# S5 output products on two halves of 64 rows, and the low weight halves of xBC and z on VectorE

## The chip, the cores and the metric

The kernel runs on one core of one Trainium2 chip. The metric is the device time of one execution in microseconds (us). Three runs of the kernel before took 1704.28, 1708.3 and 1718.86 us, so the median is 1708.3 us. The profiled execution, from which all rows below come, took 1714.9 us. Engines are named as the profile names them: PE (TensorE), DVE (VectorE), ACT (ScalarE), POOL (GpSimd) and SP (SyncE, which here only issues DMAs). Batch numbers, where the text uses them, count from 0.

## The reference, cut to what matters

One layer of a hybrid encoder on 1024 tokens of width 1024. A projection splits into z, xBC, dt and u. The columns z, xBC and dt feed a Mamba-2 group (SSD), u feeds an S5 group with 64 groups of 16 channels and 64 complex states in each direction. The two outputs are concatenated, projected, normed and added, and a SwiGLU layer follows. The change lies in the projection and the S5 part:

```
def _s5_scan(ug, lam_re, lam_im, log_dt, b_re, b_im, c_re, c_im):
    ...
    bu_re = jnp.einsum("blgh,gph->blgp", ug, bb_re)
    bu_im = jnp.einsum("blgh,gph->blgp", ug, bb_im)
    ...
    _, _, h_re, h_im = lax.associative_scan(_complex_linear_combine,
                                            (a_re, a_im, bu_re, bu_im), axis=1)
    return jnp.einsum("blgp,ghp->blgh", h_re, c_re) - jnp.einsum("blgp,ghp->blgh", h_im, c_im)

def _s5_mixer(u, ...):
    y_f = _s5_scan(ug, lam_re[0], ...)
    y_b = jnp.flip(_s5_scan(jnp.flip(ug, 1), lam_re[1], ...), 1)
    y = (y_f + y_b).reshape(bsz, seq, D_S5) + d_skip * u
    g = jax.nn.gelu(y)
    return g * jax.nn.sigmoid(g @ glu_w + glu_b)
```

## The kernel before, in words

Every large product is done in three products of split operands: a weight block `raw` of 128 x 1024 is split into a high half `whi` (a cast on ACT, L265) and a low half `wlo` (a subtraction, L266), and `gemm` runs high by high, high by low and low by high, 48 matmuls of 512 columns for a block of 128 output channels. Where the subtraction runs is set by the string `pl` in the table `KN`: it holds X and Z, so the 12 xBC blocks and the 8 z blocks take it on POOL, all others on DVE. `ensure(i + 1)` at the head of each block emits the split of the block after it.

S5 is done in chunks of 8 tokens, so the scan has 128 chunks (index k). `s_batch` makes the chunk inputs of all groups and writes them into the tile `SH` (L559). `rec_step(j)` (L617 to L629) then runs the recurrence over chunks, for both directions at once: four DVE instructions of 128 elements per row (`rn`, `rm`, `rn`, `SH`), each step on the result of the step before, 127 steps. SH is laid out with the chunk outside and the 64 values of a chunk (two components, 32 groups) next to each other. Its rows hold two groups of 64 states each (j = 0, 1).

While the recurrence runs, a loop over 18 blocks (9 of xBC, one of dt, 8 of z) emits for each block: the split of the next one, the matmuls, 8 recurrence steps, a piece of the convolution (`conv_taps`, four DVE instructions at L722, and `conv_silu` on ACT), and near the end of the loop the first pieces of the S5 output stage. All of this is under a manual schedule: each engine executes its instructions in the order in which the code emits them.

The S5 output stage (the loop over i in 16 batches of 4 groups, behind the recurrence) gives each batch three products per group, summed in PSUM (`y_mm`, L778 to L780): the within-chunk kernel `W0` times the input U, and the carried states of each direction times `cp`. The pieces are:

- `c_open`, `c_dir` (L663 to L673): cp, the output matrix times powers of the diagonal. For the first four batches on POOL (`pcd`), later on DVE.
- `k_mm`, `k_out` (L690 to L698): the within-chunk kernel, from cp and `yk`; it is copied by ACT to `lg`, gets the skip term on POOL, and goes to DRAM (`k_d`).
- `w0_load` (L704): reads it back in Toeplitz form into W0. These DMAs, and those into k_d, are issued on POOL's queue.
- `restack` (L768): a product over 128 rows needs both components of one group in the rows, and SH has two groups there. Eight copies per batch (seven on ACT, one on DVE for the first 11 batches) move SH into the tile `AH`, 128 copies in all.
- `y_out`, `g_store`: GELU on ACT, and the result to DRAM (`g_d`), from which the GLU product behind it reads.

Of the kernel before, what the change touches and what calls it, by code (L numbers as in the profile page):

```python
# [18 lines left out]
def _ap(t, off, dims):  # L19
# [63 lines left out]
 'pl': 'XZ',  # L83
# [47 lines left out]
def hymba_block(ctx, tc, P, out, dbg=None, upto=99):  # L131
# [44 lines left out]
    y12_d = dram([2, 128, 2, 1024 + 16], "y12_d")  # L176
    x12_d = dram([2, 128, 1024], "x12_d")
    k_d = dram([32, 64 * 240], "k_d")
# [110 lines left out]
    arR = rep.tile([128, 8, 128], F32, name="arR")  # L289
    aiR = rep.tile([128, 8, 128], F32, name="aiR")  # L290
# [117 lines left out]
    def s5_prep():  # L408
# [43 lines left out]
        for j in range(2):  # L452
            sl = slice(64 * j, 64 * j + 64)
            srcr = arR[sl, 7, :].rearrange("p (d q j) -> p d q j", d=2, j=2)[:, :, :, j]
# [28 lines left out]
        zp = pp.tile([128, 16], F32, name="zp")  # L483
        pool.memset(zp, 0.0)
        for y in range(2):
# [10 lines left out]
            gq.dma_start(y12_d[y][:, :, 0:1024], st.rearrange("p d g h -> p d (g h)"))  # L496
            with tc.issue_after(pows[7].ins):
                gq.dma_start(y12_d[y][:, :, 1024:1040], zp.unsqueeze(1).to_broadcast([128, 2, 16]))
# [5 lines left out]
        for y in range(2):  # L504
            st = pp.tile([128, 64, 16], F32, tag="n5", name="xst")
            for q in range(2):
                t = ptmp()
                for j in range(8):
                    h = 8 * q + j
                    pe.transpose(t[:, 64 * j:64 * j + 64], cc[:, h, y:y + 2, :].rearrange("p a b -> p (a b)"), ident[:64, :64])  # L510
                act.copy(st[:, :, 8 * q:8 * q + 8].rearrange("p g h -> p h g"), t.rearrange("p (h g) -> p h g", h=8))
            (gq if KN['xq'] else aq).dma_start(x12_d[y], st.rearrange("p g h -> p (g h)"))
# [17 lines left out]
    def s_batch(b, U):  # L530
# [12 lines left out]
        for hb in range(2):  # L543
# [6 lines left out]
            for q in range(2):  # L550
                t = ptmp()
                for d in range(2):
                    for comp in range(2):
                        for j in range(2):
# [4 lines left out]
                act.copy(SH[:, :, :, :, pq].rearrange("p d k c -> p d c k"),  # L559
                         t.rearrange("p (d c k) -> p d c k", d=2, c=2))  # L560
# [83 lines left out]
    def xt_load(b):  # L644
        if b in xts_:
            return
        g0 = 4 * b
        xt = xts_[b] = ck.tile([128, 2, 4, 16], F32, tag="xtc", name="xtc", bufs=2)
        (gq if b < KN["xtb"] else sp).dma_start(xt.rearrange("p y g h -> p y (g h)"), x12_d.rearrange("y p f -> p y f")[:, :, 16 * g0:16 * g0 + 64])
        yk = yks[b] = ck.tile([128, 2, 80], F32, tag="yk", name="yk", bufs=3)  # L650
        (gq if b < KN["xtb"] else sp).dma_start(yk, y12_d[0][:, :, 16 * g0:16 * g0 + 80])

    @pri("cb")
    def c_batch(b):
        c_open(b)
        for d in range(2):
            c_dir(b, d)

    def c_open(b):
        xt = xts_[b]  # L660
        pl = (ck, 4) if b % 7 < 4 else (yp, 3)
        cp = cps[b] = pl[0].tile([128, 2, 4, 9, 16], F32, tag="cp", name="cp", bufs=pl[1])
        act.copy(_ap(cp, 0, [[576 + 128, 2], [144, 4], [1, 16]]), xt[:, 0].unsqueeze(1).to_broadcast([128, 2, 4, 16]))  # L663

    def c_dir(b, d):
        g0 = 4 * b
        e = pool if 2 * b + d in KN['pcd'] else dve
        xt, cp = xts_[b], cps[b]
        tm = ck.tile([128, 4, 8, 16], F32, tag="tmc", name="tmc")
        dst = _ap(cp, 16 if d == 0 else 576 + 112, [[144, 4], [16 if d == 0 else -16, 8], [1, 16]])  # L670
        e.tensor_tensor(dst, spread(xt[:, 0], 8), pw4(arR, d, 1, 8, g0, 4), op=MUL)
        e.tensor_tensor(tm, spread(xt[:, 1], 8), pw4(aiR, d, 1, 8, g0, 4), op=MUL)
        e.tensor_tensor(dst, dst, tm, op=ADD)  # L673
# [3 lines left out]
    @pri("kb")  # L677
    def k_batch(b):
        k_mm(b)
        k_out(b)  # L680

    def k_mm(b):
        yk = yks[b]
        cp = cps[b]
        t = kts[b] = ptmp()
        for g in range(4):
            y0, y1 = yk[:, 0, 16 * g:16 * g + 32], yk[:, 1, 16 * g:16 * g + 32]
            for o, n, st, rhs, a, z in ((0, 8, y1, cp[:, 1, g, 1:9], True, False), (7, 1, y0, cp[:, 0, g, 0:1], False, True),
                                        (8, 7, y0, cp[:, 0, g, 1:8], True, True)):
                pe.matmul(t[32 * g:32 * g + 32, 16 * o:16 * o + 16 * n], st, rhs.rearrange("p n h -> p (n h)"),  # L690
                          start=a, stop=z, tile_position=(0, 32 * g))

    def k_out(b):
        g0 = 4 * b
        lg = ck.tile([128, 15, 16], F32, tag="lg", name="lg", bufs=2)
        act.copy(lg.rearrange("p n h -> p (n h)"), kts[b][:, 0:240])
        pool.tensor_tensor(lg[:, 7, :], lg[:, 7, :], dd[:, b, :], op=ADD)
        gq.dma_start(k_d[:, 240 * g0:240 * g0 + 960].rearrange("h (g f) -> g h f", g=4), lg.rearrange("p n h -> p (n h)"))  # L698
# [52 lines left out]
    AHs = []  # L751

    @pri("rs")
    def restack(b):

        while len(AHs) < 2:
            AH = yp.tile([128, 2, 4, 128], F32, name=f"AH{len(AHs)}")
            pool.memset(AH[:, 0, :, 0:1], 0.0)
            pool.memset(AH[:, 1, :, 127:128], 0.0)
            AHs.append(AH)  # L760
        AH, p0 = AHs[b % 2], 2 * b
        for d in range(2):
            for j in range(2):
                for comp in range(2):
                    src = SH[64 * j:64 * j + 64, d, (0 if d == 0 else 1):(127 if d == 0 else 128), comp, p0:p0 + 2]
                    dst = AH[64 * comp:64 * comp + 64, d, :, (1 if d == 0 else 0):(128 if d == 0 else 127)]
                    dst = dst.rearrange("p (q j) k -> p q j k", j=2)[:, :, j, :].rearrange("p q k -> p k q")
                    (dve.tensor_copy if 4 * d + 2 * j + comp >= 8 - KN["rsd" if b < 11 else "rse"] else act.copy)(dst, src)  # L768

    yts = {}  # L770

    def y_mm(b):
        U, W0, cp, AH = Us_[b // 2], W0s[b], cps[b], AHs[b % 2]
        c = b % 2
        t = yts[b] = ptmp()
        for g in range(4):
            o = t[:, 128 * g:128 * g + 128]
            pe.matmul(o, W0[:, 240 * g:240 * g + 128], U[:, 4 * c + g, :], start=True, stop=False)  # L778
            pe.matmul(o, cp[:, 0, g, 1:9, :].rearrange("p n h -> p (n h)"), AH[:, 0, g, :], start=False, stop=False)
# [1185 lines left out]
```

## Time and profile before

| What | Value |
|---|---|
| median of three runs | 1708.3 us (1704.28 to 1718.86) |
| profiled execution: time, span from the first to the last instruction | 1714.9 us, 1713.2 us |
| PE, PE weight loads | 91% and 74% of the span |
| DVE, ACT, POOL | 74%, 42% and 34% of the span |
| granted TensorE clock, mean | 0.956 of full speed |
| last recurrence step begins, last S5 output product begins | 444.4 us, 551.0 us |

How to read it: the shares are means over stages that differ. PE is the busiest engine overall, but in the two stages of the change, the recurrence (from 212.0 us) and the S5 output stage behind it, other engines can set the pace, and those stages must be read by themselves.

### The profile page before, as it was taken

How to read it: one execution, taken by the hardware profiler on the slowest of the kernel's cores; microseconds unless marked ns; L12 is line 12 of the kernel's file. 1: busy time of each engine (PE TensorE's matmuls, PEld its weight loads, DVE VectorE, ACT ScalarE, POOL GpSimd, SP SyncE). 2: the span in 40 equal slices, each digit the busy share in tenths (PEclk: the TensorE clock that was granted, in tenths of full speed). 3: DMA queues.
4: the chain of work that ended last, by engine and by line, in shares of the span. 5: the costliest groups of instructions: out<-in, count | busy, mean ns of one | idle time of the engine just before them, and what ended most of it. 6: DMA issues, size and time to landing. Idle time of an engine off the chain costs nothing.

```text
span 1713.2 us, 22320 instructions
## 1 busy us (share of the span) xinstructions
PE 1560.2 (91%) x7980; PEld 1272.9 (74%) x7980; DVE 1268.8 (74%) x2012; ACT 712.4 (42%) x1182; POOL 579.3 (34%) x517
## 2 busy tenths in 40 slices
PE   7998999889776879999999986999999999999897
PEld 6777788668675666778877774788888888787686
DVE  7445589999762577877577499878688788669777
ACT  6345632121697445444343255322222233344352
POOL 2101121156121020112111176545555555229512
PEclk9999999989898889999999898999999999999999
DMA  5644344243687748777578891323332231592234
GB/s 179 155 119 116 116 151 136 80 128 108 149 211 170 212 128 274 242 242 254 176 233 276 270 282 56 117 93 119 122 105 99 92 105 55 184 344 80 92 104 179
DMA packets 250146, 272.13 MB, mean 159 GB/s; under 512 B 29403, under 2 KB 190675, under 8 KB 250035
## 3 DMA queue, kind: packets, MB, share of 16 engines
q1 hardware_dynamic: 224659, 216.48, 41.2%
q0 software_dynamic: 12896, 33.83, 6.2%
q10 hardware_dynamic: 12480, 20.39, 3.4%
q8 instruction: 63, 1.03, 0.3%
q14 instruction: 48, 0.39, 0.1%
HBM read 185.76 MB, written 84.84 MB: 158 GB/s over the span
## 4 chain that ended last, share of the span: by engine, by line
PE 40%; DVE 10%; DMA 8%; issue 3%; POOL 3%; ACT 2%; SPq 0%; DVEq 0%; POOLq 0%; ACTq 0%
PE acc L1548 13%; PE ptmp L1548 9%; PE acc L1135 4%; PE ptmp L1852 4%; PE acc L1852 3%; DVE dop L1834 2%; PE acc L275 2%; DMA m<-m_d 2%; POOL wd L1819 1%; PE ptmp L954 1%; DMA m_d<-m 1%; PE ptmp L1020 1%; DMA cat<-ch_d 1%; PE ptmp L1006 1%; DMA graw<-g_d 1%
## 5 line engine op out<-in xcount | busy, mean ns | idle before, releaser
L275 PE MATMUL acc<-hTh,whi 128*128 128x512 f32 (+1 forms) x456 | 180.6, 397 | 8.2 <-ACT whi L265 8.0
L1135 PE MATMUL acc<-ohi,cat 128*128 128x512 f32 x512 | 176.3, 411 | 11.0 <-DMA cat<-ch_d 7.6
L275 PE MATMUL acc<-hTh,wlo 128*128 128x512 f32 (+1 forms) x456 | 179.3, 394 | 2.4 <-POOL wlo L266 2.3
L275 PE MATMUL acc<-hTl,whi 128*128 128x512 f32 (+1 forms) x456 | 180.2, 396 | 0.8 <-DVE hTl L335 0.8
L1531 DVE TENSOR_TENSOR wop<-rawp,wop 128x512 fp32r<-128x512 f32 x120 | 135.1, 1127 | 22.2 <-ACT wop L1530 21.1
L1548 PE MATMUL ptmp<-T,wop 128*128 128x512 f32 x528 | 127.8, 398 | 7.1 <-DVE T L1705 4.7
L1548 PE MATMUL acc<-T,wop 128*128 128x512 f32 x528 | 127.9, 398 | 3.7 <-DVE T L1705 3.7
L1852 PE MATMUL ptmp<-dop 128*128 128x512 f32 x528 | 123.9, 396 | 2.9 <-DVE dop L1834 2.9
L1135 PEld LDWEIGHTS acc<-ohi,cat 128*128 128x128 f32 x512 | 100.2, 196 | 35.0 <-DMA cat<-ch_d 8.5
L266 POOL TENSOR_TENSOR wlo<-raw,whi 128x1024 fp32r<-128x1024 f32 x20 | 50.1, 2505 | 221.2 <-ACT whi L265 221.1
L1548 PE MATMUL acc<-B,wop 128*128 128x512 f32 x528 | 124.3, 391 | 0.0
L1548 PEld LDWEIGHTS ptmp<-T,wop 128*128 128x128 f32 x528 | 101.1, 192 | 30.1 <-DVE T L1705 5.1
L1548 PEld LDWEIGHTS acc<-T,wop 128*128 128x128 f32 x528 | 100.9, 192 | 27.1 <-DVE T L1705 4.5
L1852 PEld LDWEIGHTS ptmp<-dop 128*128 128x128 f32 x528 | 101.5, 193 | 24.9 <-DVE dop L1834 3.2
L1548 PEld LDWEIGHTS acc<-B,wop 128*128 128x128 f32 x528 | 99.0, 188 | 21.5
L275 PEld LDWEIGHTS acc<-hTh,whi 128*128 128x128 f32 x456 | 87.5, 192 | 27.2 <-ACT whi L265 8.4
L1834 DVE TENSOR_TENSOR dop<-da,dop 128x512 fp32r<-128x512 f32 x77 | 76.7, 996 | 38.9 <-ACT dop L1833 38.9
L1563 ACT ACTIVATE cg<-cg 128x512 f32<-128x512 f32 x44 | 27.8, 633 | 185.1 <-DVE cg L1561 185.1
L1569 POOL TENSOR_TENSOR cg<-cg 128x512 f32<-128x512 f32 x44 | 62.0, 1409 | 125.5 <-DVE cg L1564 124.8
L275 PEld LDWEIGHTS acc<-hTh,wlo 128*128 128x128 f32 x456 | 87.3, 191 | 22.2 <-POOL wlo L266 4.2
L1135 PE MATMUL acc<-olo,cat 128*128 128x512 f32 x256 | 103.6, 405 | 0.0
L1530 ACT CAST wop<-rawp 128x512 fp32r<-128x512 f32 x120 | 70.3, 615 | 76.6 <-POOL rawp L1505 51.0
(365 smaller groups left out, 3601.8 us busy)
## 6 DMA issues: line engine op xcount, KB each, us to landing
ff_d<-cg POOLq DMA_DIRECT2D x77, 256.0 KB, 2.3
da<-ff_d SPq DMA_DIRECT2D x35, 512.0 KB
raw<-in_w_in_dram SPq DMA_DIRECT2D x28, 512.0 KB
cat<-ch_d SPq DMA_DIRECT2D x48, 256.0 KB
cat<-cl_d SPq DMA_DIRECT2D x48, 256.0 KB
wd<-in_w_down_dram SPq DMA_DIRECT2D x44, 256.0 KB
rawp<-in_w_gate_dram SPq DMA_DIRECT2D x10, 1024.0 KB
rawp<-in_w_up_dram SPq DMA_DIRECT2D x10, 1024.0 KB
```

The costliest lines, as they stand in the source:

```text
L266: (pool if ("0" if j < 2 else "A" if j < XBC0 else "X" if j < Z0 else "Z" if j < GL0 else "G" if j < FF0 else "F") in KN['pl'] else dve).t ...
L275: pe.matmul(ps, a[:, k, :], b[:, k, sl], start=(k == 0 and n == 0), stop=(k == 7 and n == 2))
L954: pe.matmul(t[:, 256 * s + 128 * d:256 * s + 128 * d + 128], Bt[:, c, g, :], Xw[:, d, c].rearrange("p h e -> p (h e)"), start=True, stop=True)
L1006: pe.matmul(yd[64 * hh:64 * hh + 64, 128 * j:128 * j + 128], X[:, c, 64 * hh:64 * hh + 64], Ms[hh][:, j, :], start=True, stop=True)
L1135: pe.matmul(ps, c[:, a, k % 4, :], b[:, k % 2, :], start=(k == 0 and n == 0), stop=(k == n_ - 1 and n == 2))
L1530: act.copy(t[:, 0], src)
L1531: dve.tensor_tensor(t[:, 1], src, t.bitcast(F32)[:, 0], op=SUB)
L1548: pe.matmul(ps, a[:, ai, k, :], b[:, bi, k, :], start=(k == 0 and q == 0), stop=(k == 3 and q == 2))
L1563: act.activation(cg[:, 0], cg[:, 0], AF.Silu)
L1569: pool.tensor_tensor(dst, a, b, op=op)
L1834: dve.tensor_tensor(t[:, k, 1], src, t.bitcast(F32)[:, k, 0], op=SUB)
L1852: pe.matmul(ps, t[:, 0, a, 128 * j:128 * j + 128], t[:, 1, b, :], start=(q == 0 and n == 0), stop=(q == NP - 1 and n == 2))
```

## The change

SH is laid out anew, with the chunk inside: `[direction, component, 32 groups, 128 chunks]`. The carried states of one group then lie side by side in 64 rows, and `y_mm` multiplies them from there: for each direction, component and j one product over 64 rows, the even groups in rows 0 to 63 and the odd ones in rows 64 to 127, into two PSUM tiles. `restack` and AH go. `cp` holds for 64 rows two components, and `yk` is spread into a block-diagonal `ybd` by two POOL copies per batch, so that `k_mm` still contracts over 128 rows. A batch now has 8 groups, so there are 8 batches; `w0_load` of a batch stands right behind its own `k_out`. All of `c_dir` is on DVE, with compact power tables `arP`, `aiP`. `pl` is empty, so all low halves are on DVE.

```
- 'pl': 'XZ',
+ 'pl': '',
...
-                act.copy(SH[:, :, :, :, pq].rearrange("p d k c -> p d c k"),
-                         t.rearrange("p (d c k) -> p d c k", d=2, c=2))
+                act.copy(SH[:, :, :, pq, :], t.rearrange("p (d c k) -> p d c k", d=2, c=2))
...
-            return _ap(SH, 64 * k + (32 if swap else 0),
-                       [[8192 + 64 * (127 - 2 * k), 2], [-32 if swap else 32, 2], [1, 32]])
+            return _ap(SH, k + (4096 if swap else 0),
+                       [[8192 + 127 - 2 * k, 2], [-4096 if swap else 4096, 2], [128, 32]])
...
+        for j in range(2):
+            sl = slice(64 * j, 64 * j + 64)
+            q.dma_start(xt[sl].rearrange("p a q h -> p a (q h)"),
+                        x3_d.rearrange("(a s) j f -> j s a f", a=3)[j][:, :, 64 * B:64 * B + 64])
+            for d in range(2):
+                q.dma_start(yk[sl, d].rearrange("p c q h -> p c (q h)"),
+                            y12p_d.rearrange("(c s) d j f -> d j s c f", c=2)[d, j][:, :, 64 * B:64 * B + 64])
+        for j in range(2):
+            sl = slice(64 * j, 64 * j + 64)
+            pool.tensor_copy(yb[sl, :, :, :, j, :].rearrange("p d c q h -> p (d c q) h"),
+                             yk[sl].rearrange("p d c q h -> p (d c q) h"))
...
-        e = pool if 2 * b + d in KN['pcd'] else dve
...
+        for c in range(2):
+            tm = ck.tile([128, 4, 8, 16], F32, tag="tmc", name="tmc")
+            dst = _ap(cp, 1152 * d + 576 * c + (16 if d == 0 else 112), [[144, 4], [16 if d == 0 else -16, 8], [1, 16]])
+            dve.tensor_tensor(dst, spread(xt[:, c], 8), pw(arP), op=MUL)
+            dve.tensor_tensor(tm, spread(xt[:, c + 1], 8), pw(aiP), op=MUL)
+            dve.tensor_tensor(dst, dst, tm, op=ADD)
...
+        for q in range(4):
+            for d in range(2):
+                o, k0, n0 = (1, 0, 1) if d == 0 else (0, 1, 0)
+                for c in range(2):
+                    for j in range(2):
+                        sl = slice(64 * j, 64 * j + 64)
+                        pe.matmul(t[j][:, 128 * q + o:128 * q + o + 127],
+                                  cp[sl, d, c, q, n0:n0 + 8, :].rearrange("p n h -> p (n h)"),
+                                  SH[sl, d, c, 4 * B + q, k0:k0 + 127], start=False, stop=(q == 3 and d == 1 and c == 1),
+                                  skip_group_check=True)
...
+        for B in range(8):
+            y_mm(B)
+            if B + 2 < 8:
+                k_mm(B + 2)
+            if B + 3 < 8:
+                c_open(B + 3)
+                c_dir(B + 3, 0)
+            if B + 2 < 8:
+                k_out(B + 2)
+                w0_load(2 * B + 4)
+                w0_load(2 * B + 5)
+            y_out(B)
```

How the instructions stand now. First DVE in the recurrence, behind a piece of the convolution (`cacc`); `rn`, `rm` and `SH` are the four instructions of a step. Before:

```order
L722 SCALAR_TENSOR_TENSOR cacc<-xpad,vec_428,cacc 128x1023 x2
L722 SCALAR_TENSOR_TENSOR cacc<-xpad,vec_428,cacc 128x1022
L626 TENSOR_TENSOR rn<-rcB,SH 128x128
L627 TENSOR_TENSOR rm<-rcA,SH 128x128
L628 TENSOR_TENSOR rn<-rn,SH 128x128
L629 TENSOR_TENSOR SH<-rm,rn 128x2x64
```

On DVE at the same place with the change:

```order
L738 SCALAR_TENSOR_TENSOR cacc<-xpad,vec_434,cacc 128x1023 x2
L738 SCALAR_TENSOR_TENSOR cacc<-xpad,vec_434,cacc 128x1022
L268 TENSOR_TENSOR wlo<-raw,whi 128x1024
L639 TENSOR_TENSOR rn<-rcB,SH 128x128
L640 TENSOR_TENSOR rm<-rcA,SH 128x128
L641 TENSOR_TENSOR rn<-rn,SH 128x128
L642 TENSOR_TENSOR SH<-rm,rn 128x2x64
```

The low half of the next weight block now stands on DVE ahead of each 8 steps, 14 of them between the first and the last step; the last one, of the last z block, stands right behind the last step:

```order
L642 TENSOR_TENSOR SH<-rm,rn 128x2x64
L268 TENSOR_TENSOR wlo<-raw,whi 128x1024
L694 TENSOR_TENSOR cp<-xtc,arP 128x4x128
L695 TENSOR_TENSOR tmc<-xtc,aiP 128x512
L696 TENSOR_TENSOR cp<-cp,tmc 128x4x128
```

So the matmuls of the last z block, and all of PE behind them, come behind the end of the recurrence on DVE.

Then POOL's queue in the S5 output stage, where `lg` is the skip term, `k_d` the store of a batch's kernel and `W` the load of W0. Before, the load behind a store is that of an earlier batch:

```order
L697 TENSOR_TENSOR lg<-lg,dd 128x16
L698 DMA k_d<-lg 4x32x240
L704 DMA W_4132<-k_d 128x1x848
L697 TENSOR_TENSOR lg<-lg,dd 128x16
L698 DMA k_d<-lg 4x32x240
L704 DMA W_4182<-k_d 128x1x848
```

On POOL with the change:

```order
L713 TENSOR_TENSOR lg<-lg,dd 128x16
L714 DMA k_d<-lg 8x16x240
L720 DMA W_4228<-k_d 128x1x848
L720 DMA W_4230<-k_d 128x1x848
L674 COPY ybd_2072<-yk 64x16x16 x2
L713 TENSOR_TENSOR lg<-lg,dd 128x16
L714 DMA k_d<-lg 8x16x240
```

The two loads now read what the store just ahead of them writes, and the two copies into `ybd` stand behind them.

Last PE in that stage. Before, the last of a batch's four groups, then the first kernel products of a later batch:

```order
L778 MATMUL ptmp<-Uy,W_4095 128x128
L779 MATMUL ptmp<-AH_4081,cp 128x128
L780 MATMUL ptmp<-AH_4081,cp 128x128
L690 MATMUL ptmp<-cp,yk 32x128
L690 MATMUL ptmp<-cp,yk 32x16
L690 MATMUL ptmp<-cp,yk 32x112
```

PE with the change, one batch of 8 groups:

```order
L777 MATMUL ptmp<-Uy,W_4595 128x128 x4
L777 MATMUL ptmp<-Uy,W_4597 128x128 x4
L785 MATMUL ptmp<-SH,cp 128x127 x32
L706 MATMUL ptmp<-cp,ybd_2073 32x128 x8
L706 MATMUL ptmp<-cp,ybd_2073 32x16 x8
L706 MATMUL ptmp<-cp,ybd_2073 32x112 x8
```

For 8 groups there were 24 products over 128 rows, and there are now 8 over 128 rows and 32 over 64 rows.

## Rows read from the trace of the kernel before

**Rows 1.** Busy time by stretch, recurrence then output stage: us, busy (instructions) per engine, PEclk, DMA.

```profile
238.47:444.70 206.23, 184.38 (x857) 147.68 (x855) 197.69 (x497) 47.19 (x66) 70.16 (x55) 0.95 0.39 118
444.70:551.00 106.30, 77.06 (x717) 70.18 (x718) 52.54 (x85) 96.35 (x170) 23.31 (x40) 0.89 0.77 187
```

**Rows 2.** Lines L629 and L780: ns min/median/max, first and last start us.

```profile
L629 DVE TENSOR_TENSOR SH<-rm,rn x127: 283/292/2911, 216.2 to 444.4; 128x128 f32<-128x128 f32 x127
...
L780 PE MATMUL ptmp<-AH,cp x128: 275/275/553, 447.7 to 551.0; 128*128 128x128 f32 x128
```

**Rows 3.** Timeline from 242.6 us: start us, us, engine, line.

```profile
242.97 2.46 POOL L266 TENSOR_TENSOR wlo<-raw,whi 128x1024 fp32r<-128x1024 f32 x1 [8.15 <-ACT whi L265]
...
243.10 2.48 DVE L628 TENSOR_TENSOR rn<-rn,SH 128x128 f32<-128x128 f32 x1
...
245.94 0.29 DVE L626 TENSOR_TENSOR rn<-rcB,SH 128x128 f32<-128x128 f32 x1
...
247.00 0.29 DVE L626 TENSOR_TENSOR rn<-rcB,SH 128x128 f32<-128x128 f32 x1
```

**Rows 4.** Groups by line and form: count, busy us, mean ns, idle before.

```profile
L768 ACT COPY AH<-SH 64x254 f32<-64x254 f32 x117 | 74.5, 637 | 15.2 <-DVE SH L629 12.8
...
L627 DVE TENSOR_TENSOR rm<-rcA,SH 128x128 f32<-128x128 f32 x127 | 58.2, 458 | 0.0
L266 POOL TENSOR_TENSOR wlo<-raw,whi 128x1024 fp32r<-128x1024 f32 x20 | 50.1, 2505 | 221.2 <-ACT whi L265 221.1
L629 DVE TENSOR_TENSOR SH<-rm,rn 128x128 f32<-128x128 f32 x127 | 50.0, 394 | 4.4
L626 DVE TENSOR_TENSOR rn<-rcB,SH 128x128 f32<-128x128 f32 x127 | 48.8, 384 | 4.1
L628 DVE TENSOR_TENSOR rn<-rn,SH 128x128 f32<-128x128 f32 x127 | 46.6, 367 | 0.0
...
L266 DVE TENSOR_TENSOR wlo<-raw,whi 128x1024 fp32r<-128x1024 f32 x24 | 29.3, 1222 | 11.6 <-ACT whi L265 11.5
...
L673 DVE TENSOR_TENSOR cp<-cp,tmc 128x512 f32<-128x512 f32 x24 | 16.7, 694 | 0.8
```

**Rows 5.** Same view: instructions with and without hops between elements.

```profile
L265 ACT CAST whi<-raw 128x1024 fp32r<-128x1024 f32 x44 | 46.0, 1045 | 33.2 <-PE acc L275 22.4 <-DMA raw<-in_w_in_dram 5.8 <-DMA raw<-in_s_glu_w_dram 2.8
...
L559 ACT COPY SH<-ptmp 128x512 f32<-128x512 f32 x32 | 32.1, 1101 | 16.8 <-PE ptmp L556 14.7 <-DMA u_d<-up 2.1
...
L549 ACT COPY bm<-ptmp 128x512 f32<-128x512 f32 x32 | 18.3, 601 | 22.2 <-PE ptmp L548 22.2
...
L1039 DVE SCALAR_TENSOR_TENSOR hl<-yg,vec,hl 128x1024 fp32r<-128x1024 f32 x8 | 18.0, 2256 | 4.0 <-issue 2.9 <-ACT hl L1038 1.1
```

**Rows 6.** The chain that ended last: one block of 48 matmuls of 512 columns.

```profile
1162.37 10.98 PE acc L1548 x48
```

**Rows 7.** PE timeline from 454.1 us: first and last of a batch, then kernel products.

```profile
454.16 0.49 PE L778 MATMUL ptmp<-Uy,W 128*128 128x128 f32 x2
...
456.72 0.39 PE L780 MATMUL ptmp<-AH,cp 128*128 128x128 f32 x2
457.03 1.41 PE L690 MATMUL ptmp<-cp,yk 128*32 128x128 f32 x24
```

**Rows 8.** Groups by line and form: products in pairs of 64 output rows.

```profile
L556 PE MATMUL ptmp<-U,bm 128*64 128x128 f32 x512 | 35.1, 284 | 1.7 <-ACT bm L549 1.7
```

**Rows 9.** DMA issues from 428 to 435 us, then 440 to 551: median us to landing last.

```profile
W<-k_d POOLq DMA_DIRECT2D x2, 424.0 KB, 10.4
...
W<-k_d POOLq DMA_DIRECT2D x14, 424.0 KB, 7.6
...
k_d<-lg POOLq DMA_DIRECT2D x13, 120.0 KB, 4.9
```

**Rows 10.** POOL timeline from 428 us: skip term and store of a batch's kernel.

```profile
449.55 0.21 POOL L697 TENSOR_TENSOR lg<-lg,dd 128x16 f32<-128x16 f32 x1 [13.68 <-ACT lg L696]
450.06 0.72 POOL L698 DMA_DIRECT2D k_d<-lg  x1 [0.30 <-POOL lg L697]
```

More of the change, by code (lines that the diff above doesn't have):

```diff
@@ L642, in hymba_block, with xt_load @@
     xts_, yks = {}, {}
-    def xt_load(b):
-        if b in xts_:
+    def xt_load(B):
+        if B in xts_:
             return
[L647 to L651, printed above, removed]
@@ L675, in hymba_block @@
-    kts = {}
[L677 to L691, printed above, removed]
@@ L693, in k_out @@
-    def k_out(b):
-        g0 = 4 * b
+        q = gq if B < 2 else sp
+        xt = xts_[B] = ck.tile([128, 3, 4, 16], F32, tag="xtc", name="xtc", bufs=2)
+        yk = ck.tile([128, 2, 2, 4, 16], F32, tag="yk", name="yk", bufs=1)
+        yb = yks[B] = ybd[B % 2]
+        for j in range(2):
[5 more added lines that the diff above has]
+                            y12p_d.rearrange("(c s) d j f -> d j s c f", c=2)[d, j][:, :, 64 * B:64 * B + 64])
@@ new lines, in hymba_block, with k_mm @@
+    kts = {}
+    def k_mm(B):
+        yb, cp = yks[B], cps[B]
+        t = kts[B] = ptmp()
+        for o, n, d, n0, a, z in ((0, 8, 1, 1, True, False), (7, 1, 0, 0, False, True), (8, 7, 0, 1, True, True)):
+            for c in range(2):
+                for q in range(4):
+                    pe.matmul(t[32 * q:32 * q + 32, 16 * o:16 * o + 16 * n], yb[:, d, c, q].rearrange("p j h -> p (j h)"),
+                              cp[:, d, c, q, n0:n0 + n].rearrange("p n h -> p (n h)"),
+                              start=a and c == 0, stop=z and c == 1, tile_position=(0, 32 * q))
@@ L770, in hymba_block @@
[L770 to L779, printed above, removed]
-            pe.matmul(o, cp[:, 1, g, 0:8, :].rearrange("p n h -> p (n h)"), AH[:, 1, g, :], start=False, stop=True)
@@ L782, in y_out, with y_mm @@
-    @pri("yo")
-    def y_out(b):
-        B, c = b // 2, b % 2
-        if c == 0:
-            Gs[B] = yp.tile([128, 8, 128], F32, tag="G", name="G", bufs=2)
-        act.activation(Gs[B][:, 4 * c:4 * c + 4, :].rearrange("p g k -> p (g k)"), yts[b], AF.Gelu_apprx_tanh)
+    yts = {}
+    def y_mm(B):
+        U, cp = Us_[B], cps[B]
+        t = yts[B] = [ptmp(), ptmp()]
+        for q in range(4):
+            W0 = W0s[2 * B + q // 2]
+            for j in range(2):
+                g = 2 * (q % 2) + j
+                pe.matmul(t[j][:, 128 * q:128 * q + 128], W0[:, 240 * g:240 * g + 128], U[:, 2 * q + j, :],
+                          start=(q == 0), stop=False, skip_group_check=True)
+        for q in range(4):
+            for d in range(2):
+                o, k0, n0 = (1, 0, 1) if d == 0 else (0, 1, 0)
+                for c in range(2):
+                    for j in range(2):
[4 more added lines that the diff above has]
+                                  skip_group_check=True)
@@ L789, in g_store, with y_out @@
+    def y_out(B):
+        G = Gs[B] = yp.tile([128, 8, 128], F32, tag="G", name="G", bufs=2)
+        for j in range(2):
+            act.activation(G.rearrange("p (q j) k -> p j q k", j=2)[:, j], yts[B][j].rearrange("p (q k) -> p q k", q=4),
+                           AF.Gelu_apprx_tanh)
     @pri("gst")
@@ L1259, in hymba_block @@
     rst = newstack()
+    ybd = [ck.tile([128, 2, 2, 4, 2, 16], F32, name=f"ybd{i}") for i in range(2)]
+    for t in ybd:
+        pool.memset(t, 0.0)
     xt_load(0)
@@ L1307, in hymba_block @@
             if 0 <= b < 4:
-                c_open(b)
-                c_dir(b, 0)
-                run_steps(KN["r3"])
-                c_dir(b, 1)
-            if 0 < b < 4:
-                k_batch(b - 1)
-            if 0 <= b + 1 < 5 and n < NB - 1:
-                xt_load(b + 1)
+                if b % 2 == 0:
+                    c_open(b // 2)
+                c_dir(b // 2, b % 2)
+            if b == 2:
+                k_mm(0)
+                k_out(0)
+            if b in (0, 3):
+                xt_load(1 if b == 0 else 2)
         run_steps(127)
-        if KC == 4:
-            xt_load(4)
         next(cvs, None)
@@ new lines, in hymba_block @@
+        for B in range(8):
[10 more added lines that the diff above has]
+            y_out(B)
+            if B + 3 < 8:
+                c_dir(B + 3, 1)
+            for b_, l in qs:
+                g_store(b_, l, Q[KN["gs"][l]])
+            qs = [(B, l) for l in range(8)]
+            if B + 4 < 8:
+                xt_load(B + 4)
+            if B + 3 < 8:
+                u_load(B + 3)
```

156 lines of the change are left out of this document (60 added, 96 removed).

## The prediction, made before the run

> **What bounds the kernel now.** I read the busy time by stretch first, then the lines, and then the single places in the timeline. In the recurrence DVE is busy for 197.69 of 206.23 us, more than any other engine, and the last step begins at 444.4 us [rows 1, 2]. PE follows closely (184.38 us), so a gain on DVE alone is soon capped. Much of DVE's time is not work: with all of POOL quiet a step takes 1.06 us, four instructions of 285 to 290 ns, while the means over 127 steps are 384, 458, 367 and 394 ns [rows 3, 4]. The timeline shows where the rest is lost. During a `wlo` on POOL of 2.46 us one DVE instruction took 2.48 us instead of 0.29 [rows 3]: DVE is held while POOL works. The excess is 127 x (94 + 173 + 82 + 104 ns) = 57.5 us.
>
> In the output stage ACT is busy for 96.35 of 106.30 us and PE for 77.06 [rows 1]; 74.5 us of ACT in all go to the restacking copies [rows 4], most of them here. The DMA engines are at 0.77 there, which is 82 us of work. So without the copies the next bounds are DMA at some 82 us, PE at 77, or a chain of dependent steps.
>
> **Holds that go, work that comes (recurrence).** The 57.5 us of holds go with `wlo` and `c_dir` on POOL. What comes on DVE between the first and the last step:
> - 14 `wlo`, at the 1222 ns of the same operation on DVE less some holds in that mean, 1.14 us each: +16 us.
> - Six `c_dir` instructions for each of the first four halves, 24 of them, at 694 ns less holds, 0.65 us each [rows 4]: +15.6 us.
> - New holds: POOL keeps issuing DMAs at 0.72 us each [rows 10], now six for each of two `xt_load` and one store of k_d, and gets the copies into `ybd`. Together I take 7 us; if a DMA issue holds DVE for none of its time, 2 us.
>
> The sum so far is -57.5 + 16 + 15.6 + 7 = -19 us.
>
> **Hops (recurrence).** Each of the four instructions of a step has one operand in SH. Before, 32 values lie side by side; now each of the 128 elements is 512 bytes from the next. No row shows DVE doing this, so I bound it. The lower bound is 0: a step is four dependent instructions of 0.29 us for 128 elements, and at DVE's slope between 512 and 1024 elements, (1222 - 694)/512 = 1.03 ns, more than half of that is not elements and might cover slower reads. A gain is excluded, since the element count stays. The upper bound is L1039, a DVE instruction that reads with hops of 32 bytes: 2256 ns against 1222 for 1024 elements [rows 4, 5], 1.01 ns more for each, 129 ns for an instruction and 66 us for 508. Between them: ACT writes 512 elements with hops of 256 bytes in 1101 ns and without in 601, and its slope without is (1045 - 601)/512 = 0.87 ns [rows 5]. So it needs 0.87 + 0.98 = 1.85 ns for a hopped element. If DVE needs the same, its extra is about 0.8 ns, 100 ns for an instruction, and 508 x 100 = +50 us. I take that, since the hop of ACT's row (256 bytes) is the nearest in size and its total per element lies inside DVE's bounds.
>
> A page of the Trainium skill has a price for this: "Vector Engine (DVE) Microarchitecture Reference", the section on measured stream behaviour on trn2, gives 1.73 ns per column when one source hops 4 KiB with every element, against 1.054 without, and more for smaller steps. By it the extra would be an estimated 0.68 x 128 = 87 ns or more, and the sum 44 us or more in place of 50. Its rule that pairs of adjacent words suffice for full rate speaks against the new layout as L1039 does.
>
> The end of the recurrence therefore moves by -19 + 50 = **+31 us** (bounds -19 and +47), to about 475.7 us. PE cannot cover this, since DVE was the busier engine already.
>
> **The last z block (between the stages).** Its `wlo` now stands behind the last step on DVE, and all later PE work stands behind its matmuls. Before, PE was free and waited for the last step. Now it gets 1.2 us of `wlo` and a block of 48 matmuls, 10.98 us [rows 6], before the first output product: +12 us, to 487.8. Before, the first product on carried states began about 3 us behind the last step, when ACT had restacked (the last of the batch begins at 447.7 [rows 2]).
>
> **The output stage.** ACT loses its copies, and its remaining work (GELU, `lg`, `cp`) fits beside the rest. On PE a matmul instruction takes 0.112 us: 24 of them fill the 2.56 us between the first and the last of a batch, with two instructions for each product [rows 7]. A batch of 8 groups has 16 such over 128 rows (1.8 us) and 64 over 64 rows. No row has pairs over 64 rows. The bounds for one are 0.056 us, if two halves run fully side by side, and 0.112, if they don't at all: 5.4 and 9.0 us for a batch. The nearest row is L556, pairs over 64 columns, 512 products in 35.1 us busy, 0.069 us each [rows 8]. I take that: 1.8 + 64 x 0.069 = 6.2 us. The kernel products of a batch, 1.41 us for 24 instructions [rows 7], become 48 narrow ones, of which I take 2.3 us.
>
> A page of the Trainium skill, "TensorEngine Tiling (Array Packing)", says under its overview that two tiles of 64 rows give up to twice the speed. By it alone a batch would be at 5.4 us; what switching between whole and half rows costs no run here shows.
>
> PE thus needs 8.5 us for a batch, 68 us for eight. But W is now loaded straight behind its own store. POOL's queue waits there for the store; the copies into `ybd` and the next skip term stand behind it, but they are wanted a batch later. For batch B + 2 the chain is: k products behind y of batch B (2.3), ACT's copy and the skip term (about 1.0; the add is 0.21 us [rows 10]), k_d to landing 4.9, the two W loads 9.5, then y of B + 2 (6.2). The 9.5 lies between 7.6 for a single load, the lower bound, and 10.4 for two together plus an issue of 0.6 [rows 9]. That is 23.9 us for two batches, above PE's 17. W of batch 1 uses the buffers of the last z block, so its loads start at about 488 and land at 498 (10.4). From there three periods and one y: 498 + 3 x 23.9 + 6.2 = 576 us, against 551.3 before. The stage becomes about 88 us behind the start of its products, but starts 43 us behind the old end of the recurrence.
>
> **First part.** Up to 212 us the change adds two reordering copies and compact power tables (some 3 us on DVE) and takes away holds of five `wlo`; ACT's write into SH is without hops now, up to 0.5 us less for each of 32 [rows 5]. I count 0, between -4 and +4.
>
> **Sum.** 576 - 551.3 = +24.5 us, on 1714.9 us of the profiled execution. That one stood 6.6 us above the median, so the forecast is 1708.3 + 24 = **1732 us**.
>
> **Rivals.**
> 1. *Hops are covered* (the fixed part of each instruction hides them). Then the recurrence ends at -19, and the stage is 12 + 88 us behind that: 444.7 - 19 + 100 = 526 against 551.3, -25.5 us, 1683 us. For it: most of an instruction is not elements. Against it: ACT's and L1039's rows. It decides at a hop of about 0.4 ns or 50 ns an instruction, where the total is level with before. Chance 0.15.
> 2. *The W chain does not bind*, since fewer other transfers run beside the loads, and the stage falls to the DMA work of 82 us, counted from the end of the recurrence plus 3 us of start: 475.7 + 85 = 561, +9.5 us, 1717 us. For it: single loads took 7.6 us with much traffic. Chance 0.25.
> 3. *64-row products gain nothing* (9.0 us a batch). The chain's period is then 26.7 us, four y in the sum: +11 us, 1743; with a granted clock below the 0.89 of the old stage [rows 1], because PE waits in each period, 1746. For it: no row shows the pairing. Chance 0.20.
> 4. The forecast, 0.40.
>
> **Range and chances.** Upper bound of the hops gives 1748, rival 3 about 1745. The lower end lies between rivals 1 and 2: a hop at half its price gives 1732 - 25 = 1707, and I leave out only the full case of rival 1. So 1690 to 1752. A measurement of this kernel can tell about 1%, 17 us, from no change: under 1691 lies rival 1 (0.15, and little else), between 1691 and 1725.4 lie rival 2 and the cheap end of the hops (0.34), above that the rest (0.50).
>
> **What would show it.** Right: the four step instructions near 390 ns and none held for 2 us; the last step near 476 us and the last z block's matmuls behind it; output products from 488 us with PE waiting for W<-k_d in a period of some 24 us; ACT well below PE there; L785 at 0.069 us spacing. Wrong: steps still at 0.29 us (rival 1), PE dense in the output stage or DMA above 0.9 (rival 2), L785 at 0.112 us (rival 3). The whole would be wrong if DVE is held as much as before by the DMA issues that POOL keeps, or if the first part moved by more than 4 us.

## The result, and the profile after

The changed kernel took 1729.8 us (median of four runs, 1727.5 to 1738.7) against 1710.3 us for the kernel before in the same job. The ratio of the runs is 1.0139 with an interval of 1.0099 to 1.0178 (the two medians alone give 1.0114), so it is slower by 1.1 to 1.4%. The forecast of 1732 us was met to 2 us; the change itself was forecast at 24 us and measured 19.5 us. The profiled execution of the changed kernel is its slowest run, 1738.7 us; its trace is therefore read for where things lie and what waits for what, and the size of the whole is taken from the medians. Behind the last output product the twelve traces of this document take between 1154 and 1163 us, the changed kernel's the longest, so a few us between two traces are no result.

The total hides two parts that were both off by about 20 us, in opposite directions. The places in the trace show it. Busy time by stretch, now cut at the last step and at the first output product (columns as in [rows 1]):

```profile
238.47:453.40 214.93, 171.20 (x760) 134.98 (x759) 206.86 (x507) 42.04 (x55) 1.96 (x4) 0.90 0.27 89
453.40:465.45 12.05, 12.05 (x55) 9.77 (x54) 6.57 (x11) 1.49 (x3) 2.05 (x4) 1.00 0.81 185
465.45:573.60 108.15, 72.57 (x975) 67.73 (x975) 42.51 (x65) 20.15 (x38) 20.35 (x37) 0.79 0.80 176
```

The last recurrence step begins at 453.4 us, 9 us later than before [rows 2], where 31 were forecast. The 12 us of the last z block are there to the tenth, and PE is busy for all of them. The output stage lasts 108 us where 88 were forecast; ACT is busy for only 20 us of it, and still it is no shorter than before. The last output product begins at 573.6 us, 22.6 us later than before.

The four instructions of a step and the low halves, by line and form, answer to [rows 4]:

```profile
L268 DVE TENSOR_TENSOR wlo<-raw,whi 128x1024 fp32r<-128x1024 f32 x44 | 53.9, 1226 | 15.3 <-ACT whi L267 15.3
L642 DVE TENSOR_TENSOR SH<-rm,rn 128x128 f32<-128x128 f32 x127 | 49.9, 393 | 4.3
L639 DVE TENSOR_TENSOR rn<-rcB,SH 128x128 f32<-128x128 f32 x127 | 49.3, 388 | 3.8
L641 DVE TENSOR_TENSOR rn<-rn,SH 128x128 f32<-128x128 f32 x127 | 48.6, 383 | 0.0
L640 DVE TENSOR_TENSOR rm<-rcA,SH 128x128 f32<-128x128 f32 x127 | 48.6, 383 | 0.0
...
L785 PE MATMUL ptmp<-SH,cp 64*128 64x127 f32 x512 | 36.5, 307 | 0.0
...
L573 ACT COPY SH<-ptmp 128x512 f32<-128x512 f32 x32 | 18.3, 586 | 17.3 <-PE ptmp L570 15.8 <-DMA u_d<-up 1.5
```

The means look like those of before, but they say something else: before, an instruction took 284 to 292 ns (medians) and 35 of the 508 were held beyond 0.6 us, one for 5.8 us; now every instruction is near its mean. One line of the step shows it (min, median, max in ns):

```profile
L642 DVE TENSOR_TENSOR SH<-rm,rn x127: 375/389/596, 211.4 to 453.4; 128x128 f32<-128x128 f32 x127
```

The median went from 292 to 389 ns and the longest from 2911 to 596 [rows 2]. So the holds are gone, and each instruction is longer instead; that the hops are the reason is shown by the runs below. The step's period, between starts in the timeline, is 1.45 us in place of 1.06.

In the output stage the timeline of PE at its beginning (start, duration, instructions, idle time before) shows the new pace:

```profile
465.45 1.95 PE L777 MATMUL ptmp<-Uy,W 128*128 128x128 f32 x16
467.32 3.84 PE L785 MATMUL ptmp<-SH,cp 64*128 64x127 f32 x64
471.09 1.15 PE L706 MATMUL ptmp<-cp,ybd 128*32 128x128 f32 x48
481.39 2.05 PE L777 MATMUL ptmp<-Uy,W 128*128 128x128 f32 x8 [9.14 <-issue]
485.71 2.07 PE L777 MATMUL ptmp<-Uy,W 128*128 128x128 f32 x8 [2.27 <-DMA W<-k_d]
...
539.86 1.94 PE L876 MATMUL ptmp<-ident,BT 128*128 128x128 f32 x8 [9.35 <-DMA BT<-xs_d]
```

The first batch is done in 1.95 + 3.84 us, at a granted clock of 1.00, and its kernel products in 1.15; then PE waits for W of the next batch. Where the trace says "issue", the first of W's two loads had been missing: it landed at 481.3 us, and the row behind waits for the second (485.7). Over the whole stage the idle time of PE is nearly all in two places, ahead of the products with W, and in the wait for BT, the input of the second SSD group's transposes:

```profile
L777 PE MATMUL ptmp<-Uy,W 128*128 128x128 f32 x128 | 23.7, 355 | 26.2 <-issue 19.0 <-DMA W<-k_d 3.6 <-ACT Bt L877 3.5
```

The 72.57 us busy, these 26.2 and the 9.35 for BT make up the 108 us. POOL's timeline shows why W of batch 1 came so late, and the same wait for the store at batch 2:

```profile
467.87 0.51 POOL L674 COPY ybd<-yk 64x256 f32<-64x256 f32 x1 [0.25 <-DMA yk<-y12p_d]
468.39 1.17 POOL L720 DMA_DIRECT2D W<-k_d  x2
472.86 0.61 POOL L713 TENSOR_TENSOR lg<-lg,dd 128x16 f32<-128x16 f32 x1 [3.31 <-ACT lg L712]
473.77 0.62 POOL L714 DMA_DIRECT2D k_d<-lg  x1 [0.30 <-POOL lg L713]
486.85 1.17 POOL L720 DMA_DIRECT2D W<-k_d  x2 [12.46 <-DMA k_d<-lg]
```

### The profile page after: what moved, and what is told of

Same layout as the page of the kernel before. It is cut to its first block, busy times and chain, and to the rows that moved or that the text cites. A ratio compares the mean times of both kernels' runs of the same rounds, so it can differ in the third digit from the quotient of the medians.

```text
span 1737.0 us, 22677 instructions
## 1 busy us (share of the span) xinstructions
PE 1557.4 (90%) x8236; PEld 1271.7 (73%) x8236; DVE 1293.8 (74%) x2051; ACT 624.5 (36%) x1049; POOL 502.9 (29%) x474
## 3 DMA queue, kind: packets, MB, share of 16 engines
q8 instruction: 65, 1.06, 0.3%
## 4 chain that ended last, share of the span: by engine, by line
PE 41%; DVE 8%; DMA 6%; POOL 5%; issue 4%; ACT 2%; SPq 0%; POOLq 0%; DVEq 0%; ACTq 0%
PE acc L1552 13%; PE ptmp L1552 9%; PE acc L1142 5%; PE ptmp L1856 3%; POOL wd L1823 3%; PE acc L1856 2%; PE acc L277 2%; PE ptmp L1027 1%; PE ptmp L961 1%; DMA cat<-ch_d 1%; DVE dop L1838 1%; DVE cacc L738 1%; PE ptmp L1013 1%; DMA raw<-in_s_glu_w_dram 1%; DMA cl_d<-ghl 1%
## 5 line engine op out<-in xcount | busy, mean ns | idle before, releaser
L277 PE MATMUL acc<-hTh,wlo 128*128 128x512 f32 (+1 forms) x456 | 185.1, 406 | 37.8 <-DVE wlo L268 37.8
L277 PE MATMUL acc<-hTh,whi 128*128 128x512 f32 (+1 forms) x456 | 184.4, 405 | 0.4 <-ACT hTh L339 0.4
L1535 DVE TENSOR_TENSOR wop<-rawp,wop 128x512 fp32r<-128x512 f32 x120 | 137.4, 1146 | 17.9 <-ACT wop L1534 16.7
L277 PEld LDWEIGHTS acc<-hTl,whi 128*128 128x128 f32 x456 | 90.0, 197 | 19.5 <-DVE hTl L342 1.1
L1856 PE MATMUL acc<-dop 128*128 128x512 f32 x396 | 95.7, 398 | 7.5 <-DVE dop L1838 4.8
```

Of the source, the lines that this page charges most:

```text
L277: pe.matmul(ps, a[:, k, :], b[:, k, sl], start=(k == 0 and n == 0), stop=(k == 7 and n == 2))
L1535: dve.tensor_tensor(t[:, 1], src, t.bitcast(F32)[:, 0], op=SUB)
L1856: pe.matmul(ps, t[:, 0, a, 128 * j:128 * j + 128], t[:, 1, b, :], start=(q == 0 and n == 0), stop=(q == NP - 1 and n == 2))
```

## The experiments

The theory after this trace was: hops cost DVE 0.39 us a step, holds had cost 61 us, the last z block stands on the path, and the output stage is paced by the chain of store and load. The rivals were that the step is longer for another reason, that held time costs nothing, and that the stage is bound by DMA work. Ratios are to the kernel before on the same chip; that of the changed kernel itself is 1.0139 (1.0099 to 1.0178).

**One part alone: the engines.** The kernel before, with

```
- 'pl': 'XZ',  'pcd': [0, 1, 2, 3, 4, 5, 6, 7],
+ 'pl': '',    'pcd': [],
```

> The kernel before with all low halves and all of c_dir on DVE; layout, restacking copies and output stage stay as before. Theory (holds by POOL cost DVE some 61 us, the work taken over costs 31.5): no step instruction above 0.6 us, recurrence 30 us shorter on DVE, but PE's 18 blocks then set the end and the output products start only 10 to 18 us earlier: 1690 to 1700 us. Rival (the holds were time in which DVE would have waited anyway, so only the added work counts): last step later than 444 us and about 1725 us.

1697.2 us, ratio 0.9935 (0.9917 to 0.9954). The step's last instruction, columns as above:

```profile
L629 DVE TENSOR_TENSOR SH<-rm,rn x127: 281/292/294, 215.7 to 411.8; 128x128 f32<-128x128 f32 x127
```

No instruction is held, and the last step begins 33 us earlier than before. PE's blocks end at 426.7 us, 9 us earlier than before, and the stage behind still has its restacking copies (ACT 88.3 of 100.2 us busy). So the theory stands: held time on DVE was real, the work taken over cost less, and PE capped what came of it. This half of the change made the kernel faster by 11 us; the other half, on top of it, cost 33 (1729.8 - 1697.2).

**The other part alone: low halves back on POOL.** The changed kernel, with

```
- 'pl': '',
+ 'pl': 'XZ',
```

> The changed kernel with only the low halves of xBC and z put back on POOL. Theory: 14 low halves leave DVE (-16 us), but each holds one instruction by about 2 us (+28 us), so the last step is 10 to 14 us later than 453 us; the last z block no longer stands behind it, so the first product follows the last step by under 3 us in place of 12. Both together: within 5 us of the changed kernel, 1726 to 1735 us. Rival (a held instruction costs no more than the work it replaces): last step at 437 us or earlier and about 1708 us.

1740.2 us, ratio 1.0198 (1.0167 to 1.0229), slower than expected. The last instruction of the step:

```profile
L642 DVE TENSOR_TENSOR SH<-rm,rn x127: 373/389/2618, 213.0 to 476.4; 128x128 f32<-128x128 f32 x127
```

The last step came at 476.4 us, 23 us later than in the changed kernel, not 10 to 14: the steps' time, added up from the starts in the timeline, rose from 180 to 213 us, and 15 step instructions were above 0.6 us, so a hold costs 2.2 us against 1.15 for the same subtraction on DVE. Three more conv instructions between the first step and the last (5.6 us) had not been foreseen; against these stand the 16 us of low halves that left DVE. The rival, a hold no dearer than the work it replaces, is refuted. The first product came 1.5 us behind the last step, as expected.

**Hops away: the old layout.** The changed kernel with the chunk outside in SH; TensorE reads its columns 256 bytes apart.

```
- SH = shp.tile([128, 2, 2, 32, 128], F32, name="SH")
+ SH = shp.tile([128, 2, 128, 2, 32], F32, name="SH")
...
-     SH[sl, d, c, 4 * B + q, k0:k0 + 127]
+     SH[sl, d, k0:k0 + 127, c, 4 * B + q]
```

> The changed kernel with the chunk outside in SH again, so that DVE's steps read 32 values side by side and TensorE's output products read their 127 columns 256 bytes apart. Theory (hops cost DVE 0.39 us a step, 47 us in all): step period back from 1.45 to 1.06 us, PE's blocks set the end, output products start 20 to 30 us earlier, 1700 to 1712 us if TensorE reads hopped columns at its old rate; if TensorE paid 0.8 ns for each hopped column, a batch's 64-row products would take 100 ns more each (6.4 us a batch), and about half of the gain would be lost. Rival (the step is longer for another reason than the hops, for example the engine's other work): period stays at 1.45 us and the time at 1730 us.

1692.8 us, ratio 0.9915 (0.9887 to 0.9943), faster than the kernel before. The step is back at 292 ns, and the last one at 410.0 us, with everything else of the change in place:

```profile
L642 DVE TENSOR_TENSOR SH<-rm,rn x127: 283/292/295, 213.3 to 410.0; 128x128 f32<-128x128 f32 x127
...
426.90 7.20 PE L785 MATMUL ptmp<-SH,cp 64*128 64x127 f32 x64
```

So the hops are the cause of the longer step. The gain of 37 us over the changed kernel came although TensorE now pays for hops itself: its 64 products of a batch took 7.20 us in place of 3.84. In this stage it waits for W anyway. Against the engines alone (0.9917 to 0.9954) the intervals overlap: with this layout, the rest of the change is worth nothing that can be told from noise.

**Hops of pairs.** SH with two groups side by side, then the chunk, so that DVE reads pairs of adjacent words with 1 KiB between pairs, and TensorE every second word. The step's swap of components moves from SH to the contiguous `rn` and `rcB`.

```
- SH = shp.tile([128, 2, 2, 32, 128], F32, name="SH")
+ SH = shp.tile([128, 2, 2, 16, 128, 2], F32, name="SH")
...
+ def at(k):
+     return _ap(SH, 2 * k, [[8192 + 2 * (127 - 2 * k), 2], [256, 32], [1, 2]])
...
+ dve.tensor_tensor(sw(n), sw(rcB), at(j - 1), op=MUL)
```

> The changed kernel with SH laid out so that two groups lie side by side and the chunk is next: DVE's steps read pairs of adjacent words with hops of 1 KiB between them, TensorE reads every second word. Theory (each element that is not adjacent to the one before pays): if a pair costs one hop, half of 0.39 us goes, period 1.25 us and 1710 to 1722 us; if adjacent pairs run at full rate, as the Trainium skill's page Vector Engine (DVE) Microarchitecture Reference has it, period 1.06 us and the same time as with the old layout, 1700 to 1712 us. Rival (hops are not the cause): period 1.45 us.

1688.1 us, ratio 0.9893 (0.9871 to 0.9914). The time doesn't separate it from the old layout, though it does from the engines alone, by 9 us. The rows separate the two layouts, on three engines (by line and form, then the timeline):

```profile
L646 DVE TENSOR_TENSOR SH<-rm,rn 128x128 f32<-128x128 f32 x127 | 37.2, 293 | 4.4
...
L573 ACT COPY SH<-ptmp 128x512 f32<-128x512 f32 x32 | 19.8, 632 | 16.6 <-PE ptmp L570 16.6
...
424.80 3.91 PE L789 MATMUL ptmp<-SH,cp 64*128 64x127 f32 x64
```

DVE is at its contiguous rate, ACT's write within 8%, and TensorE at 3.9 us a batch. The Trainium skill's page "Vector Engine (DVE) Microarchitecture Reference" states in its section on measured stream behaviour that runs of two adjacent words, begun on an 8-byte boundary, go at full rate whatever hop lies between them. These rows agree with the Trainium skill, 293 against 292 ns.

**The chain of store and load.** The changed kernel with k products one batch further ahead, so that W's data are stored a batch before its load.

```
             y_mm(B)
+            if B + 2 < 8:
+                w0_load(2 * B + 4)
+                w0_load(2 * B + 5)
-            if B + 2 < 8:
-                k_mm(B + 2)
+            if B + 3 < 8:
+                k_mm(B + 3)
...
```

> The changed kernel with the kernel products k_mm and the store of k_d one batch further ahead, so that the loads of W for batch B + 2 stand behind the output products of batch B with their data stored a batch earlier. Theory (the output stage of 108 us is a chain of store, load and products): the landing of k_d, the copy and the k products, some 8 us of each period, leave the chain, the stage takes 85 to 98 us and the time is 1707 to 1720 us. Rival (the stage is bound by DMA work, 0.80 busy, which does not shrink): stage at least 103 us, 1725 us or more.

1719.0 us, ratio 1.0064 (1.0042 to 1.0086), 11 us faster than the changed kernel. From the first product to the last the stage took 91 us (470.3 to 561.8) in place of 108, within the theory's range:

```profile
470.33:561.80 91.47, 67.85 (x932) 63.22 (x928) 38.07 (x60) 18.21 (x36) 18.33 (x34) 0.83 0.82 188
```

The DMA engines' work in it fell as well, from some 86 us (0.80 of 108) to 75, since loads now stand ahead of the stage; by itself this run therefore doesn't exclude the rival. The last run below does: its stage reaches a share of 0.91, so 0.80 was no limit. The start came 5 us later, since the k products of batch 2 now stand ahead of it and wait for cp:

```profile
469.47 0.94 PE L706 MATMUL ptmp<-cp,ybd 128*32 128x128 f32 x40 [1.48 <-DVE cp L696]
470.33 2.05 PE L777 MATMUL ptmp<-Uy,W 128*128 128x128 f32 x16
```

**The last z block.** The changed kernel with

```
- 'r1': 8,
+ 'r1': 7,
```

> The changed kernel with 7 recurrence steps a block in place of 8, so that the last low half stands on DVE some 15 steps ahead of the last step. Theory (the last z block behind the recurrence costs 12 us on the path): the last z block ends before the last step, output products start within 3 us of it in place of 12, and everything behind moves up: 1717 to 1722 us. Rival (the stage behind is paced by transfers that do not start earlier): less than 4 us gained, 1726 us or more.

1718.8 us, ratio 1.0057 (1.0035 to 1.0079). The last low half was made at 435.7 us, the last z block ended at 447.7, and now the products waited for the recurrence, no longer for that block:

```profile
448.14 2.05 PE L777 MATMUL ptmp<-Uy,W 128*128 128x128 f32 x16
456.80 0.80 PE L785 MATMUL ptmp<-SH,cp 64*128 64x127 f32 x4 [6.61 <-DVE SH L642]
```

The gain is 11 us by the medians. But the low half behind the last step can't be its whole cause. In the changed kernel it was made just as PE finished the block ahead of it:

```profile
453.61 1.21 DVE L268 TENSOR_TENSOR wlo<-raw,whi 128x1024 fp32r<-128x1024 f32 x1
...
454.64 0.39 PE L277 MATMUL acc<-hTl,whi 128*128 128x512 f32 x1
...
454.88 0.50 PE L277 MATMUL acc<-hTh,wlo 128*128 128x512 f32 x1
```

PE lost some 0.1 us there. It had last waited at 443.85 us, for the low half before that one, and from there two blocks ran without a gap. All through the recurrence PE waits for low halves that stand among DVE's steps, and with 7 steps a block these waits shrink. First the changed kernel, then this run (us in all, times, longest):

```profile
PE acc L277 <- DVE wlo L268: 37.8, 9, 9.1
...
PE acc L277 <- DVE wlo L268: 27.8, 8, 6.1
```

So the run shows what the place of all low halves among the steps costs; no run moved the last one alone.

**Row halves side by side or not.** The changed kernel with `for j in range(2)` as the outer loop of the 64-row products, so that neighbours use the same rows.

```
-        for q in range(4):
+        for j in range(2):
             for d in range(2):
...
-                    for j in range(2):
+                    for q in range(4):
```

> The changed kernel with all products on rows 0 to 63 of a batch first and those on rows 64 to 127 behind them, so that two halves never stand next to each other but at one place. Theory (neighbours on different row halves run side by side, 64 instructions in 3.8 us): without neighbours 0.11 us each, 7.1 us for 64, 3.3 us more a batch; four batches lie on the chain, so 7 to 14 us slower, 1737 to 1744 us. Rival (a product on 64 rows is short by itself): still 3.8 us for 64, 1730 us.

1736.5 us, ratio 1.0166 (1.0132 to 1.0201), which overlaps with the changed kernel's interval, so the time is inconclusive. The row is not: the batch's 64 instructions need 7.07 us in place of 3.84.

```profile
467.66 7.07 PE L785 MATMUL ptmp<-SH,cp 64*128 64x127 f32 x64
```

Both are first batches at a granted clock of 1.00. Side by side they go 1.84 times as fast. The Trainium skill's page "TensorEngine Tiling (Array Packing)" says up to twice in its overview, and the row agrees with the Trainium skill.

**The wait for BT.** The changed kernel with the transposes of the second SSD group one batch later, behind the same load.

```
-        yield from ssd_prep(1)
+        p = ssd_prep(1)
+        yield next(p)
+        yield
+        yield from p
```

> The changed kernel with the second group's eight transposes (which wait 9.3 us for their input in TensorE's queue, behind the products of batch 5 of 8) one batch later, the load staying where it is. Theory (the chain of stores and loads of W sets the pace): W of the next odd batch lands 6 us behind the start of that wait anyway, so 2 to 4 us are gained, 1726 to 1728 us. Rival (this wait is the one on the path): 8 to 9 us, 1721 us.

1726.7 us, ratio 1.0109 (1.0080 to 1.0138), a gain of 3 us that lies inside both intervals. It is what the theory expected, but no proof. The trace adds that PE now waits at the next batch instead, until W lands (549.6):

```profile
549.67 3.75 PE L777 MATMUL ptmp<-Uy,W 128*128 128x128 f32 x16 [7.10 <-issue]
```

**All together.** The pair layout with the k products ahead and the transposes later:

> The pair layout of SH together with the kernel products one batch further ahead and the second group's transposes one batch later. Theory (the three costs lie in different places of one path): the gains of the single edits, some 11 and 3 us, come on top of the pair layout's 1688 us, with some overlap between the two: 1674 to 1680 us, faster than the kernel before by 1.6 to 2%. Rival (with the stage shorter, the DMA work in it, 0.79 busy, sets its length): 1684 us or more.

1682.4 us, ratio 0.9857 (0.9831 to 0.9883): 6 us below the pair layout alone, between the expectation and its rival, and the two intervals overlap. The stage is 11 us shorter than with the pair layout alone (88.7 us for 100.1), but begins 7 us later (430.1 for 422.9), in part because the k products of batch 2 stand ahead of it. The last z block ended at 426.0 us, 15 us behind the last step (410.9), which the next run took up: the same with 7 steps a block.

> As the run with pairs and products ahead, with 7 recurrence steps a block in place of 8. Theory (without hops TensorE, not VectorE, sets the end of the recurrence, so the last z block is not late there): no gain, within 4 us of it. Rival (the last z block is still behind DVE): 8 us or more faster.

1673.0 us, ratio 0.9805 (0.9778 to 0.9831), 9 us faster still. The expectation of no gain was wrong, and its rival right in size, but not in its reason. In the run before, the last low half was ready at 412.3 us, while PE was in the block ahead of it until 415.1; it held up nothing, and PE's last wait for one had been at 390.6. What 7 steps took away is waits for earlier low halves (run before, then this one):

```profile
PE acc L277 <- DVE wlo L268: 13.5, 7, 3.2
...
PE acc L277 <- DVE wlo L268: 4.1, 4, 1.5
```

PE's blocks end 14.6 us earlier (411.4 us), then PE waits 9.1 us for cp, and the last output product ends 3 us earlier. The rest of the gain lies behind the stage, and its cause stays open. This version is faster than the kernel before by 2%; what 7 steps would do in the kernel before, no run shows. Its output stage, from the first product on carried states to the last:

```profile
426.70:515.50 88.80, 64.72 (x914) 59.93 (x912) 39.59 (x61) 16.55 (x35) 20.25 (x36) 0.83 0.91 205
```

Now the DMA engines are at 0.91 for 88.8 us, 81 us of work: here, and in no run before (0.83 at most), the stage is near the limit of its transfers.

## Why the prediction was right, and where it was not

**What bounds the recurrence, and the holds.** Right, and a little too small. Time added up from start to start on DVE between the first and the last step: 232.4 us before, 243.0 after. Steps undisturbed at 127 x 1.057 = 134.2 us leave 61.3 us of holds and waits before (forecast 57.5), and the engines alone bring the steps to 134.1 us, so all of it goes.

**Work taken over.** 14 low halves measured 16.1 us (forecast 16), 24 `c_dir` instructions 15.4 (15.6).

**Hops.** The step went from 1.057 to 1.450 us, 98 ns an instruction in the median step; forecast 100. Over all steps the trace has 180.3 - 134.2 = 46 us (91 ns an instruction) against 50. The prediction's estimate from the Trainium skill's page "Vector Engine (DVE) Microarchitecture Reference" (measured stream behaviour), 44 us, is nearer still. ACT's write hop was a good stand-in for DVE's read hop.

**New holds of 7 us: the step that failed in the recurrence.** There were none. POOL was busy for 12.6 us between the first step and the last, 1.96 of them from 238.47 us on, and no step instruction was above 0.6 us, though POOL issued loads and a store and made copies between the steps. With the conv pieces 5.7 us shorter (three instructions of them now fall ahead of the first step), the first step 1.6 us earlier, and 4 us each from holds and hops, this makes up the 22 us between 475.7 and 453.4.

**The last z block, 12 us.** Right in size: 453.40 to 465.45 in the trace. The reason given, its low half behind the last step, is only half of it. That low half and the end of the block ahead on PE met within 0.3 us (454.83 and 454.58), since the block ahead had itself waited for its low half until 443.85. Either alone holds the first product until 465 us. The prediction named one of the two, and that they met is chance.

**The output stage: the mechanism right, the term mis-sized by 20 us.** Its chain is what paces it, as the run with stores ahead shows. The landing of W for batch 1 was put at 10.4 us behind the start of the products; it was 20.2. Of this difference 3 us came since W's loads stood on POOL behind the `ybd` copies, which wait for yk (467.87), and the rest from transfers that took 12.9 and 16.7 us; the store of k_d behind them took 12.5 against 4.9 forecast. Why transfers were so slow between 468 and 486 us stays open: they fell in the same stretch as the store of z and the loads of yk and xtc, but no run took these away; with the old layout the same two loads, issued 40 us earlier, took 12.7 and 16.4 us. From there on the trace has 88 us against 77.9: 24.9, 31.0 and 24.9 us for two batches each, where the forecast has three times 23.9, and 7.4 against 6.2 us for the last. The long period holds PE's wait for BT, 9.35 us, which stands in its queue ahead of batch 5 and which the prediction overlooked; W of that batch had landed 4.7 us before its products began. Taking the wait away gained some 3 us, inside the noise.

**PE's products.** The first batch needed 5.8 us for the 6.2 forecast, at a granted clock of 1.00. Over the eight batches it was 7.5 us on average (23.7 + 36.5 us), at a granted clock of 0.79 over the stage, a mix of the 2.4 and 1.2 GHz levels; the 64 products of one batch (from 557.3 us) took 5.57 us at a mean of 0.67, after PE had waited twice for their W. So the price was too low for the clock that the stage got, some 1 us a period. The kernel products took 1.15 us a batch for 2.3.

**The rivals.** Hops were not covered, but that case was priced well: the pair layout, which takes them away and leaves all else, came out at 1688 us where rival 1 had 1683. Rival 2 (a stage at the DMA work) did not happen in the changed kernel (0.80 busy) and came near in the last run (0.91). Rival 3 was refuted by the row of 3.84 us against 7.07 one after the other.

**The sum.** Recurrence -22, stage +20 against the forecast: that the total agreed to 2 us is chance as much as merit. The sign and the mechanisms (hops cost more than the holds gave back; the stage without copies is paced by its own stores and loads) are shown by the runs, the last of them in part by the trace alone.

## What to carry to other kernels

A layout that saves one engine its copies can charge every instruction of another: look at which engine reads the tile most often on the critical path, and lay it out so that this engine sees at least two adjacent words (293 ns for 389 here), with the strided read left to the engine that waits. When a copy stage on ACT falls away, the chain of store, load and use behind it becomes the pace, and such loads belong one batch further ahead. Work that feeds a second engine and stands among the steps of a loop on a busy one makes the second wait at every block: here one number, steps per block, was worth 9 to 11 us. And when an engine is busy without a gap where it was expected to wait, look for its last wait, however far back.

## What was not expected of the hardware

- TensorE pays for hops of its moving columns: 64 products of 127 columns took 7.20 us at 256 bytes between columns, 3.91 us at 8 bytes and 3.84 us side by side, all at a granted clock of 1.00.
- ACT's write of 512 elements took 1101 ns with hops of 256 bytes [rows 5], 632 ns with hops of 8 bytes and 586 ns without.
- DMA issues on POOL did not hold DVE's steps: with the engines alone changed, POOL issued loads and stores of 0.7 us each between the steps, and no `SH` instruction took more than 294 ns. POOL's own subtractions of 2.5 us held them for some 2.2.
